# A differential attention layer: the heads' norm factors begun behind each head, the last head's scaling issued later

## The chip, the cores and the metric

The kernel runs on one core of a Trainium2 chip. The metric is the device time of one execution in microseconds, the median of a few runs. The core's engines take their instructions in order, each from its own queue: TensorE (PE, with its weight loads, PEld), VectorE (DVE), ScalarE (ACT), GpSimd (POOL) and SyncE (SP, which issues DMAs). An instruction that waits for another engine holds everything behind it in its own queue.

## The reference

One layer of a streaming encoder for two groups with the same weights: a prompt of 512 tokens and a sample of 64 tokens, 576 in all, with width 1024. It computes

```
h = x + W_out [ GDN(n) ; DiffAttn(n) ],    n = rmsnorm(x)
h = h + MemCrossAttn(rmsnorm(h), memory K/V)
h = h + W2 relu(W1 rmsnorm(h))^2
y = rmsnorm_final(h)
```

and also gives out the new keys, values and states. GDN is a gated recurrence over chunks of 64 tokens in four heads. The part that the change touches is differential attention, four heads of width 128. A head's output for a query is `softmax(q1·k1) V − lam · softmax(q2·k2) V`, and it is then normalised over its own 128 columns:

```
a  = p[:, :, 0] - lam * p[:, :, 1]
ob = _rmsnorm(a @ v, p['diff_norm']) * (1.0 - lam_init)
_rmsnorm(x, g) = x * rsqrt(mean(x*x) + EPS) * g
```

So each query row of each head has one norm factor, `(mean of squares + EPS)^-0.5`, by which its 128 outputs are multiplied. All is in float32.

## The kernel before

**Tiling and stages.** Rows are handled in tiles of 128 partitions. Products in float32 are made of rounded high and low halves, three products each (high·high, high·low, low·high), all recorded at one line, L107 (L113 is the transpose on PE). Weights come by DMA in slabs of 128x1024 (`raw`); ACT copies the high half (L159, `wh`) and DVE subtracts it to get the low half (L160, `wl`). The stages are: norm and turning of the input, the projections and the recurrence of the prompt, then for each head of differential attention its projection (`diff_project`) and the head itself (`diff_head`), with the recurrence of the sample cut in pieces between the heads; then the projection of memory keys and values, the output projection, memory attention, the feed-forward part and the last norm.

**A head.** `diff_head` treats the 64 sample rows first (`sample_rows`, t = 4): score products into the one bank `g1`, maximum (L1055, L1056) on DVE, exponential on ACT (L1058), the weights' scaling on DVE (L1060 to L1062), a turning product with `both` on PE, and the output product into the one bank `gs`. Then the four prompt tiles t = 0 to 3 do the same with two softmaxes (maxima L1097 and L1098, combination L1102 to L1105). ACT takes the sum of squares of each output (L1114, column t of `so`) and copies the output into `on` (tag `an`, five tiles of 128x128).

**The norm of a head.** `factors()` is two instructions on POOL, a 128x5 multiply-add (L1118) and a power (helper, L206), which turn `so` into `co`. `finish()` multiplies `on` by `co` in one DVE instruction (L1127, 128x640), turns it on PE and scales it on ACT into `od`. For heads 0 to 2 `finish` is handed to the next head, which calls it as `between()` ahead of its second prompt tile (t = 1). For the last head it is called in the memory projection.

**The memory projection.** A loop over the weights of keys, then of values; for each, two halves `f` of the columns and four slabs `kc`. In slab 1 the keys of the half before are turned (`turn_keys`): twice, four transposes into a bank, then `split_turned` with a copy on ACT (L1153) and a subtraction on DVE (L1154, into `At0`, `At1`, `Dt0`, `Dt1`). The last head's `finish()` is called right behind this, at values, f = 0, kc = 1.

**What sets the order.** The program is written stage by stage, and a scheduler in the framework makes each engine's queue from it, by the order in which the code was written, by dependences, by which buffers are free, and by its own idea of how long each instruction takes. Buffers of one tag are reused in turn. `tc.issue_after(x)` holds an instruction behind instruction x in that scheduling. The order is fixed when the program is built; on the chip only waits remain.

Of the kernel before, what the change touches and what calls it, by code (L numbers as in the profile page):

```python
# [11 lines left out]
ALU = mybir.AluOpType  # L12
# [3 lines left out]
P = 128  # L16
# [8 lines left out]
H = 4  # L25
# [12 lines left out]
def hybrid_layer_kernel(  # L38
# [9 lines left out]
    nc = tc.nc  # L48
    V, A, G = nc.vector, nc.scalar, nc.gpsimd
# [33 lines left out]
    def pair(slot, dt=F32):  # L83

        return up.tile([P, 2, 4, T], dt, tag=f"u{slot}", name=nm("u"))
# [6 lines left out]
    def small(tag, shape, bufs=None, dt=F32):  # L92
        tag = SHARED.get(tag, tag)
        bufs = 1 if tag in ("vn", "on", "S", "qz") or tag[:-1] in ("At", "Dt", "Y") else 2
        return sp.tile(shape, dt, tag=tag, name=nm(tag), bufs=bufs)

    def tiny(shape, tag="tiny", bufs=16):
        return tp.tile(shape, F32, tag=tag, name=nm(tag), bufs=bufs)

    def bank(tag="ba"):  # L100
        return ps.tile([P, 512], F32, tag=tag, name=nm(tag), bufs=BANKS[tag])
# [4 lines left out]
    def mm(out, lhsT, rhs, start=True, stop=True, pin=False, skip_group_check=False):  # L106
        i = nc.tensor.matmul(out, lhsT, rhs, start=start, stop=stop, skip_group_check=skip_group_check)  # L107
        if pin:
            tc.keep_in_program_order(i)

    def tr(out, in_, pin=False):
        n = in_.shape[0]
        i = nc.tensor.transpose(out, in_, ident[:n, :n])  # L113
        if pin:
            tc.keep_in_program_order(i)
# [89 lines left out]
    def rpow(out, in_, n=None):  # L205
        G.tensor_tensor(out, in_, bc(nhalf[: in_.shape[0], 0:1], list(in_.shape)), ALU.pow)  # L206
# [419 lines left out]
    def v4(ap, nb):  # L626
        return ap.rearrange("p (h n) -> p h n", h=4)[:, :nb, :]
# [186 lines left out]
    def gdn_scan(c, L, q, S):  # L814

        (_, kb), (cq, qb) = (blocks(typ, c, L) for typ in (1, 0))
        wide = [P, 4, P]

        def each(f, tag="gs"):
            b = bank(tag)  # L820
            for h in range(H):
                f(b[:, h * P : (h + 1) * P], h)
            return v4(b, 4)

        if S is None:
            r = q["vb"]
        else:
            b = each(lambda o, h: mm(o, kb(h), S[:, h, :]))
            r = sb("r", 1)
            V.tensor_tensor(r, q["vb"], b, ALU.subtract)  # L830
        b = each(lambda o, h: mm(o, q["X"][:, h, :], r[:, h, :]))
        vn = sb("vn", 1)
        V.tensor_tensor(vn, b, q["brk"].unsqueeze(2).to_broadcast(wide), ALU.mult)

        def out(o, h):
            if S is not None:
                mm(o, qb(h), S[:, h, :], stop=False)
            mm(o, q["KQ"][:, h, :], vn[:, h, :], start=S is None)

        bo = each(out)  # L840
        b = each(lambda o, h: mm(o, q["kd"][:, h, :], vn[:, h, :]), "ba")
        S = next_state(c, S, b)
        on = sb("on", 1)
        norm = normed(q, 4, [(slice(0, P), bo)], on)
        next(norm)

        def finish():
            with tc.issue_after(summed[min(c + 2, 4)]):
                next(norm, None)
            bt = each(lambda o, h: tr(o, on[:, h, :]))  # L850
            V.scalar_tensor_tensor(cq, bt, gn, zs[:, :, L], ALU.mult, ALU.mult)

        return S, finish
# [60 lines left out]
    S, behind = None, lambda: None  # L914
    prepared = [gdn_prep(*chunks[0])]
    for c, _, L in chunks[:4]:
# [5 lines left out]
        S, behind = gdn_scan(c, L, prepared[c], S)  # L922
# [152 lines left out]
    def diff_head(h, between):  # L1075


        hs = slice(h * P, (h + 1) * P)
        so, co = tiny([P, 5], "ta"), tiny([P, 5], "ta")
        on = small("an", [P, 5, P])  # L1080
        for t in (4, 0, 1, 2, 3):
            if t == 1:
                between()
            q0 = QT[t][0]
            nk = q0 + P if t < 4 else PAST + DEC
            nb = (nk + P - 1) // P
            if t == 4:
                sample_rows(h, hs, so, on)
                continue
            pr = {}  # L1090
            mx, l = tiny([P, 2], "ta"), tiny([P, 2], "ta")
            for c in (1, 0):
                b = bank(f"g{c}")
                for j in range(2):
                    mm(b[:, :nk], qs[h % 2][:, c, q0 : q0 + P], stacked[h][c][j][:, :nk], start=j == 0, stop=j == 1)
                V.memset(b[:64, nk - 64 : nk], -1e30)
                V.tensor_reduce(mx[:, c : c + 1], b[:, :nk], AX.X, ALU.max)  # L1097
                V.tensor_scalar(mx[:, c : c + 1], mx[:, c : c + 1], -0.125, None, ALU.mult)  # L1098
                p = small(f"p{c}", [P, 512])
                A.activation(p[:, :nk], b[:, :nk], AF.Exp, bias=mx[:, c : c + 1], scale=0.125, accum_out=l[:, c : c + 1])  # L1100
                pr[c] = p
            V.reciprocal(l, l)  # L1102
            V.tensor_tensor(l[:, 1:2], l[:, 1:2], nlam, ALU.mult)
            V.tensor_scalar(pr[1][:, :nk], pr[1][:, :nk], l[:, 1:2], None, ALU.mult)
            V.scalar_tensor_tensor(pr[0][:, :nk], pr[0][:, :nk], l[:, 0:1], pr[1][:, :nk], ALU.mult, ALU.add)  # L1105
            bt = bank()
            aT = small("aT", [P, 4, P])
            for kb in range(nb):
                tr(bt[:, kb * P : (kb + 1) * P], pr[0][:, kb * P : (kb + 1) * P])
            A.copy(aT[:, :nb, :], v4(bt, nb))  # L1110
            po = bank("gs")[:, :P]
            for kb in range(nb):
                mm(po, aT[:, kb, :], vtm[:, kb, hs], start=kb == 0, stop=kb == nb - 1)
            A.activation(pr[1][:, :P], po, AF.Square, accum_out=so[:, t : t + 1])  # L1114
            A.copy(on[:, t, :], po)

        def factors():
            G.tensor_scalar(so, so, 1.0 / P, EPS, ALU.mult, ALU.add)  # L1118
            rpow(co, so)

        if h == H - 1:
            factors()

        def finish():
            if h < H - 1:
                factors()
            V.tensor_tensor(on, on, co.unsqueeze(2).to_broadcast([P, 5, P]), ALU.mult)  # L1127
            b, b2 = bank(), bank()
            for t in range(4):
                tr(b[:, t * P : (t + 1) * P], on[:, t, :])  # L1130
            tr(b2[:, :P], on[:, 4, :])
            for src, ts_ in ((b, slice(0, SEQ)), (b2[:, DEC:P], slice(SEQ, T))):
                A.activation(od[:, h, ts_], src, AF.Identity, scale=dn)

        return finish

    finish = lambda: None
    for h in range(H):
# [4 lines left out]
        finish = diff_head(h, finish)  # L1143
# [30 lines left out]
    for w, out in ((w_mem_k, o_mk), (w_mem_v, o_mv)):  # L1174
        dst = tokens
        for f in range(2):
            fs = slice(512 * f, 512 * f + 512)
            bs = [bank("pr") for _ in range(2)]
            for kc in range(4):
                wt = split_weights(w[0, 256 * kc : 256 * kc + 256, fs], [P, 2, 512])  # L1180
                if kc == 1:
                    turn_keys()
                    if out is o_mv and f == 0:
                        finish()
                for k in (2 * kc, 2 * kc + 1):
                    for t in range(2):
                        ts_ = slice(t * P, (t + 1) * P)
                        for j, (wi, x) in enumerate(((0, mh), (0, ml), (1, mh))):
                            mm(
                                bs[t], x[:, k, ts_], wt[wi][:, k % 2, :],  # L1190
                                start=(k == 0 and j == 0), stop=(k == KT - 1 and j == 2),
                            )
            for t in range(2):
                (A.copy if t else V.tensor_copy)(dst[:, t, fs], bs[t])
                if out is o_mv:
                    A.copy(mv[:, t, fs], dst[:, t, fs])
                    V.tensor_tensor(mvl[2 * t + f], dst[:, t, fs], mv[:, t, fs].bitcast(F32), ALU.subtract)
            nc.sync.dma_start(out[0, 0].rearrange("(b p) h d -> p b (h d)", p=P)[:, :, fs], dst[:, :, fs])
            turn_keys = key_turns(f, dst) if out is o_mk else lambda: None
            if out is o_mv and f == 0:  # L1200
                ob = pair(5, F32R)
                for h in range(H):
                    split_to((ob,), od[:, h, :], h, 0)
# [513 lines left out]
```

## Time and profile before

| | us |
|---|---|
| runs | 977.66, 977.60, 976.36 |
| median | 977.60 |
| profiled execution | 977.09 |
| its span | 975.3 |
| PE busy | 960.4 (98%) |
| DVE busy | 689.4 (71%) |
| ACT busy | 536.9 (55%) |
| POOL busy | 66.6 (7%) |

The span is the time between the first and the last instruction of the profiled execution. Busy time is the union of an engine's instructions; the TensorE clock was granted in full. A row of the timeline gives start and duration in us, the engine, the line, the operation with output and inputs by the program's names, and in brackets the idle time ahead of it on its engine with the instruction that ended it. Rows with `x2` and more stand for that many instructions of a kind, one after the other.

### The profile page before, as it was taken

What the parts mean: (1) busy time and instruction counts of PE and PEld (TensorE: products, weight loads), DVE (VectorE), ACT (ScalarE), POOL (GpSimd) and SP (SyncE); (2) the same over time, 40 slices, a digit from 0 to 9 for tenths busy, and PEclk for the clock granted to TensorE, in tenths of its full rate; (3) what the DMA queues carried; (4) which work ended last, traced back from release to release, by engine and by line L of the source; (5) the groups of instructions that cost most, each with busy time, mean ns of one, the idle gap of its engine ahead of it and who ended that gap; (6) DMA issues with size and microseconds to landing.
All of it is one profiled execution on the core that took longest, in us unless ns stands there. A gap on an engine that the chain in (4) does not pass through costs nothing.

```text
span 975.3 us, 16991 instructions
## 1 busy us (share of the span) xinstructions
PE 960.4 (98%) x6399; PEld 889.9 (91%) x6399; DVE 689.4 (71%) x1508; ACT 536.9 (55%) x1218; POOL 66.6 (7%) x158
## 2 busy tenths in 40 slices
PE   9999999998999999999999999999999999999996
PEld 7999998997888878999999999999999999999996
DVE  6655777776867776666657888567867779978674
ACT  6664774533656765435445567665544444545444
POOL 4341020211010000000000000000000000000000
PEclk9999999999999999999999999999999999999999
DMA  7442332120744666341121423332323223322202
GB/s 209 117 138 77 95 125 66 46 64 23 187 122 122 219 182 196 87 130 44 45 65 44 141 69 96 90 88 88 87 81 87 87 87 87 87 87 87 66 23 97
DMA packets 124915, 96.01 MB, mean 98 GB/s; under 512 B 6204, under 2 KB 112846, under 8 KB 124322
## 3 DMA queue, kind: packets, MB, share of 16 engines
q1 hardware_dynamic: 124466, 94.28, 33.6%
q8 instruction: 50, 0.82, 0.4%
q10 hardware_dynamic: 368, 0.66, 0.2%
q14 instruction: 31, 0.25, 0.1%
HBM read 79.93 MB, written 9.75 MB: 92 GB/s over the span
## 4 chain that ended last, share of the span: by engine, by line
PE 58%; issue 2%; DVE 1%; ACT 1%; DMA 0%; POOLq 0%; POOL 0%; ACTq 0%; DVEq 0%; SPq 0%
PE pr L107 37%; PE ba L107 10%; PE g L107 6%; PE gs L107 4%; PE ba L113 1%; DMA raw<-in_w_ff_dram 0%; ACT u L1596 0%; ACT c L1504 0%; DVE u L1552 0%; DVE w2l L1458 0%; ACT c L1503 0%; DVE w L1357 0%; DVE wl L1357 0%; DVE wh L1357 0%; ACT wl L1356 0%
## 5 line engine op out<-in xcount | busy, mean ns | idle before, releaser
L107 PE MATMUL pr<-u,wh 128*128 128x320 f32 (+2 forms) x1240 | 325.9, 341 | 0.1
L107 PE MATMUL pr<-u,wl 128*128 128x256 f32 (+1 forms) x816 | 226.1, 301 | 0.0
L107 PEld LDWEIGHTS pr<-u,wh 128*128 128x128 f32 x1240 | 212.1, 189 | 15.2 <-ACT u L286 0.3
L107 PEld LDWEIGHTS pr<-u,wl 128*128 128x128 f32 x816 | 150.5, 189 | 2.5 <-DVE wl L387 0.2
L160 DVE TENSOR_TENSOR wl<-raw,wh 128x1024 fp32r<-128x1024 f32 x65 | 79.5, 1223 | 56.5 <-ACT wh L159 56.3
L159 ACT CAST wh<-raw 128x1024 fp32r<-128x1024 f32 x65 | 68.2, 1049 | 61.9 <-PE pr L107 46.6
L107 PE MATMUL pr<-u,w2h 128*128 128x320 f32 (+1 forms) x384 | 98.5, 341 | 0.0
L1457 ACT CAST w2h<-r 128x512 fp32r<-128x512 f32 x56 | 34.7, 620 | 87.6 <-PE pr L107 85.4
L107 PE MATMUL pr<-f,w2h 128*128 128x320 f32 (+1 forms) x288 | 74.5, 341 | 0.5 <-DVE u L1546 0.5
L107 PEld LDWEIGHTS pr<-u,w2h 128*128 128x128 f32 x384 | 65.0, 188 | 4.5 <-ACT u L1542 0.3
L107 PE MATMUL pr<-u,w2l 128*128 128x256 f32 (+1 forms) x256 | 65.2, 296 | 0.0
L1544 DVE TENSOR_TENSOR u<-u,pr 128x256 f32<-128x256 f32 x96 | 42.4, 450 | 17.1 <-PE pr L107 16.5
L206 POOL TENSOR_TENSOR tiny<-tiny,nhalf 128x1 f32<-128x1 f32 (+4 forms) x10 | 8.8, 879 | 651.3 <-DVE tiny L1610 514.1
L107 PE MATMUL ba<-u,wl 128*128 128x288 f32 x360 | 52.9, 296 | 0.0
L107 PEld LDWEIGHTS pr<-f,w2h 128*128 128x128 f32 x288 | 48.8, 188 | 4.5 <-issue 1.7
L107 PEld LDWEIGHTS ba<-u,wl 128*128 128x128 f32 x360 | 49.2, 188 | 0.6 <-ACT keep L1494 0.5
L107 PE MATMUL pr<-f,w2l 128*128 128x256 f32 (+1 forms) x192 | 48.9, 295 | 0.0
L107 PEld LDWEIGHTS pr<-u,w2l 128*128 128x128 f32 x256 | 47.0, 189 | 1.5
L1458 DVE TENSOR_TENSOR w2l<-r,w2h 128x512 fp32r<-128x512 f32 x56 | 38.5, 688 | 9.6 <-ACT w2h L1457 9.4
L107 PE MATMUL pr<-wh,u 128*128 128x512 f32 x128 | 41.6, 400 | 0.1
L1503 ACT ACTIVATE c<-c 128x288 f32<-128x288 f32 x48 | 20.6, 443 | 28.5 <-DVE c L1502 28.5
L107 PEld LDWEIGHTS pr<-f,w2l 128*128 128x128 f32 x192 | 35.2, 189 | 1.1
(552 smaller groups left out, 2024.8 us busy)
## 6 DMA issues: line engine op xcount, KB each, us to landing
raw<-in_w_ff_dram SPq DMA_DIRECT2D x36, 512.0 KB
raw<-in_w_in_dram SPq DMA_DIRECT2D x28, 512.0 KB
r<-in_w_ff_dram SPq DMA_DIRECT2D x56, 256.0 KB
raw<-in_w_mem_k_dram SPq DMA_DIRECT2D x8, 512.0 KB
raw<-in_w_mem_v_dram SPq DMA_DIRECT2D x8, 512.0 KB
raw<-in_w_out_dram SPq DMA_DIRECT2D x8, 512.0 KB
raw<-in_w_mem_q_dram SPq DMA_DIRECT2D x8, 512.0 KB
raw<-in_w_mem_o_dram SPq DMA_DIRECT2D x8, 512.0 KB
```

What stands on the lines that cost most here:

```text
L107: i = nc.tensor.matmul(out, lhsT, rhs, start=start, stop=stop, skip_group_check=skip_group_check)
L113: i = nc.tensor.transpose(out, in_, ident[:n, :n])
L159: A.copy(wh, raw)
L160: V.tensor_tensor(wl, raw, wh.bitcast(F32), ALU.subtract)
L206: G.tensor_tensor(out, in_, bc(nhalf[: in_.shape[0], 0:1], list(in_.shape)), ALU.pow)
L1457: A.copy(wh, src)
L1458: V.tensor_tensor(wl, src, wh.bitcast(F32), ALU.subtract)
L1503: A.activation(c, c, AF.Relu)
L1544: V.tensor_tensor(am, am, b, ALU.add)
```

## The change

`factors()` is called at the end of every head, not only of the last; `finish()` holds only the scaling and what follows. `finish` has an argument: where it is given, the scaling on DVE is issued behind that instruction. The last head's call gives the newest instruction of the program at that place, which is the second subtraction of `turn_keys`.

```diff
@@ -1118,13 +1118,11 @@
             G.tensor_scalar(so, so, 1.0 / P, EPS, ALU.mult, ALU.add)
             rpow(co, so)
 
-        if h == H - 1:
-            factors()
-
-        def finish():
-            if h < H - 1:
-                factors()
-            V.tensor_tensor(on, on, co.unsqueeze(2).to_broadcast([P, 5, P]), ALU.mult)
+        factors()
+
+        def finish(behind=None):
+            with tc.issue_after(behind) if behind is not None else ExitStack():
+                V.tensor_tensor(on, on, co.unsqueeze(2).to_broadcast([P, 5, P]), ALU.mult)
             b, b2 = bank(), bank()
             for t in range(4):
                 tr(b[:, t * P : (t + 1) * P], on[:, t, :])
@@ -1181,7 +1179,7 @@
                 if kc == 1:
                     turn_keys()
                     if out is o_mv and f == 0:
-                        finish()
+                        finish(nc.cur_bb.bb.instructions[-1])
```

No instruction is added or removed on any engine. Lines behind the edit have numbers smaller by two (the scaling is L1125, the subtraction of `split_turned` L1152). Since the scheduler works from the code's order, the queues of PE, DVE, ACT and SP come out in another order from the end of head 0 to the turning of the last head's output; from the first product of the output projection on they are alike. On POOL one thing moves: head 0's power stands ahead of the four POOL instructions of the sample's recurrence, where it stood behind them.

The names in the rows below carry a number each: `an` is `on`, the tile that is scaled, `ta` holds the small columns (`so`, `co`, maxima and sums), `p0` and `p1` are softmax weights, `g0` and `g1` score banks, `pr` banks of projections, `ba` other banks, `u` shared tiles.

DVE at the end of head 1, before: from the reciprocal of the next head's sample rows (it stands right behind L1105 of this head's last tile) to the scaling.

```order
L1060 RECIPROCAL ta_630_3570<-ta_630_3570 128x1
L1061 TENSOR_TENSOR ta_630_3570<-ta_630_3570,nlam_2540 64x1
L1096 MEMSET g1_639_3597 64x64
L1062 TENSOR_SCALAR p1_632_3576<-p1_632_3576,ta_630_3570 128x320
L901 SCALAR_TENSOR_TENSOR on_593_3341<-gs_625_3560,gcol_378,u_2_76 128x256
L903 TENSOR_TENSOR u_425_2518<-on_593_3341,u_425_2518 128x4x64
L1006 COPY u_4_78<-pr_692_3838 128x320
L1097 TENSOR_REDUCE ta_637_3595<-g1_639_3597 128x1
L160 TENSOR_TENSOR wl_766_4135<-raw_764_4132,wh_765_4134 128x1024
L1098 TENSOR_SCALAR ta_637_3595<-ta_637_3595 128x1
L1097 TENSOR_REDUCE ta_637_3595<-g0_641_3605 128x1
L1127 TENSOR_TENSOR an_546_3170<-an_546_3170,ta_545_3169 128x640
```

The same place in the change, right behind L1105 of the head's last tile:

```order
L1055 TENSOR_REDUCE ta_629_3571<-g1_631_3573 128x1
L1125 TENSOR_TENSOR an_546_3172<-an_546_3172,ta_545_3171 128x640
L1006 COPY u_4_78<-pr_692_3840 128x320
L901 SCALAR_TENSOR_TENSOR on_593_3343<-gs_625_3562,gcol_378,u_2_76 128x256
L160 TENSOR_TENSOR wl_766_4135<-raw_764_4132,wh_765_4134 128x1024
L903 TENSOR_TENSOR u_425_2518<-on_593_3343,u_425_2518 128x4x64
L1056 TENSOR_SCALAR ta_629_3571<-ta_629_3571 128x1
L982 TENSOR_TENSOR vb_678_3744<-u_4_78,kd_677_3743 128x256
L1060 RECIPROCAL ta_630_3572<-ta_630_3572 128x1
L1061 TENSOR_TENSOR ta_630_3572<-ta_630_3572,nlam_2540 64x1
L193 TENSOR_TENSOR zr_699_3906<-pr_698_3889,zr_699_3906 128x256
L1062 TENSOR_SCALAR p1_632_3578<-p1_632_3578,ta_630_3572 128x320
```

The scaling has moved up past the weight subtraction and the work on the next head's sample rows, so that L1056 and L1060 to L1062 stand behind it, with the weight subtraction L160 between them. At heads 0 and 2 it stands right behind L1055 as well.

PE at the end of head 1, before, behind the scores of this head's tiles: the products of the next head's scores, `g1_639`, and then the last tile's turning and output.

```order
L107 MATMUL g1_639_3597<-Dt0_600_3355,qs_430_2543 128x128
L107 MATMUL g1_639_3597<-Dt1_601_3356,qs_430_2543 128x128
L113 MATMUL ba_590_3327<-ident_79,p0_589_3321 128x128 x4
L113 MATMUL ba_611_3444<-ident_79,u_4_78 128x128 x2
L107 MATMUL pr_692_3838<-u_7_92,wl_688_3808 128x320
L107 MATMUL pr_692_3838<-u_7_92,wh_687_3807 128x320 x2
L107 MATMUL pr_692_3838<-u_7_92,wl_688_3808 128x320
L107 MATMUL gs_592_3334<-u_4_78,aT_591_3328 128x128 x4
```

In the change, `g1_639` stands here, some thirty rows further down the queue, behind 21 projection products that come after the last tile's output:

```order
L107 MATMUL pr_701_3913<-u_6_91,wh_696_3885 128x320 x2
L107 MATMUL g1_639_3599<-Dt0_600_3357,qs_430_2543 128x128
L107 MATMUL g1_639_3599<-Dt1_601_3358,qs_430_2543 128x128
L107 MATMUL pr_701_3913<-u_6_91,wl_697_3886 128x320
L107 MATMUL pr_701_3913<-u_6_91,wh_696_3885 128x320 x2
L107 MATMUL pr_701_3913<-u_6_91,wl_697_3886 128x320
L107 MATMUL ba_633_3584<-both_2546,p1_632_3578 128x128 x3
```

`ba_633`, the turning of the next head's sample weights, has moved with it, from ahead of these projection products to behind them.

DVE at the last head, before:

```order
L160 TENSOR_TENSOR wl_791_4280<-raw_789_4277,wh_790_4279 128x1024
L1154 TENSOR_TENSOR At0_754_4122<-ba_784_4233,u_753_4121 128x512
L1127 TENSOR_TENSOR an_706_3948<-an_706_3948,ta_705_3947 128x640
L200 TENSOR_TENSOR u_810_4403<-u_2_76,u_810_4403 128x576
L1154 TENSOR_TENSOR At1_755_4123<-ba_785_4240,u_753_4121 128x512
L160 TENSOR_TENSOR wl_796_4303<-raw_794_4300,wh_795_4302 128x1024
L1194 COPY u_2_76<-pr_776_4207 128x512
```

and in the change:

```order
L160 TENSOR_TENSOR wl_806_4363<-raw_804_4360,wh_805_4362 128x1024
L1152 TENSOR_TENSOR At0_754_4122<-ba_784_4233,u_753_4121 128x512
L200 TENSOR_TENSOR u_810_4403<-u_2_76,u_810_4403 128x576
L1152 TENSOR_TENSOR At1_755_4123<-ba_785_4240,u_753_4121 128x512
L1152 TENSOR_TENSOR Dt0_756_4124<-ba_800_4324,u_753_4121 128x512
L160 TENSOR_TENSOR wl_809_4381<-raw_807_4378,wh_808_4380 128x1024
L1152 TENSOR_TENSOR Dt1_757_4125<-ba_801_4331,u_753_4121 128x512
L1125 TENSOR_TENSOR an_706_3950<-an_706_3950,ta_705_3949 128x640
```

The scaling (on `an_706`) has moved behind the last split of turned keys (`Dt1_757`), and the splits of the second half of the keys, `Dt0` and `Dt1`, stand closer to those of the first.

## The prediction

> **What bounds the kernel now.** I read the page's table of busy time first, then the chain of waits, then the stretch in which the order of instructions changes (272 to 381 us: from the end of head 0 to the first product of the output projection), as a view by windows (start:end, length, then busy us of PE, PEld, DVE, ACT and POOL, granted clock, DMA share, GB/s).
>
> ```profile
> PE 960.4 (98%) x6399; PEld 889.9 (91%) x6399; DVE 689.4 (71%) x1508; ACT 536.9 (55%) x1218; POOL 66.6 (7%) x158
> PE 58%; issue 2%; DVE 1%; ACT 1%; DMA 0%; POOLq 0%; POOL 0%; ACTq 0%; DVEq 0%; SPq 0%
> 272.00:381.00 109.00, 107.26 (x621) 91.03 (x621) 74.89 (x197) 68.80 (x192) 7.02 (x14) 1.00 0.57 171
> ```
>
> PE is busy for 98% of the span and most of the chain that can be followed is PE. In the stretch PE stands idle for 109.00 − 107.26 = 1.74 us at a granted clock of 1.00. No instruction is added or removed, so two things can happen only: idle PE time goes away (1.74 us at most, 0.18% of the time) or new idle time comes in. Gains are capped, losses are not. DVE, busy 74.89 of 109.00 us, has slack on the average; what counts is whether one of its instructions that PE waits for comes late.
>
> **The last head: a wait taken away.** Its lines in the timeline are (start, duration, engine, line, operation; in brackets the idle time ahead and what ended it):
>
> ```profile
> 352.88 1.16 POOL L206 TENSOR_TENSOR ta<-ta,nhalf 128x5 f32<-128x5 f32 x1
> 354.08 0.83 DVE L1127 TENSOR_TENSOR an<-an,ta 128x640 f32<-128x640 f32 x1 [1.97 <-POOL ta L206]
> 356.09 1.22 DVE L160 TENSOR_TENSOR wl<-raw,wh 128x1024 fp32r<-128x1024 f32 x1
> 357.22 0.68 DVE L1194 COPY u<-pr 128x512 f32<-128x512 f32 x1
> 355.36 0.62 PE L107 MATMUL pr<-wh,u 128*128 128x512 f32 x2
> 356.04 0.61 PE L107 MATMUL pr<-wh,u 128*128 128x512 f32 x2
> 357.36 0.50 PE L107 MATMUL pr<-wl,u 128*128 128x512 f32 x1 [0.71 <-DVE wl L160]
> 357.96 0.73 PE L107 MATMUL pr<-wh,u 128*128 128x512 f32 x2
> ```
>
> The scaling L1127 stands in DVE's queue until POOL has the power at 354.04; DVE idles 1.97 us. Behind it come two splits and a weight subtraction (L160), which ends at 357.31, and PE's product of that low half starts at 357.36. PE's groups of three products follow each other in 0.68 us (355.36 to 356.04), 0.228 each, so the product would have come at 356.04 + 2 × 0.228 = 356.50 without the wait: 0.86 lost. The next pair comes at 357.96 instead of 357.36 + 0.23 = 357.59: 0.37. Together **1.23 us**, the most that can come back. In the change the scaling stands behind the last split, some 4 us later, and waits for nothing; but the second pair of splits moves ahead of it and the two banks of turned keys are then still worked off one after the other, so I leave about 0.3 lost: **−0.9** (bounds −1.25 and 0: nothing, if another wait on DVE stands there instead).
>
> **Heads 0 to 2: a wait added.** By program order, POOL's two instructions now come ahead of the next head's work, and by the queues the scaling moves up with them: it stands right behind the next head's first maximum (heads 1 and 2: L1055; head 0: likewise), where before it stood some ten instructions later and waited for nothing. DVE works in order, so whatever is behind it waits for POOL. Head 1, before:
>
> ```profile
> 302.14 0.54 ACT L1058 ACTIVATE p<-g,ta 128x320 f32<-128x320 f32 x1
> 302.22 0.75 DVE L1105 SCALAR_TENSOR_TENSOR p<-p,ta,p 128x512 f32<-128x512 f32 x1
> 302.83 0.44 PE L107 MATMUL g<-Dt,qs 128*128 128x128 f32 x2 [0.18 <-ACT p L1058]
> 303.49 0.39 DVE L1062 TENSOR_SCALAR p<-p,ta 128x320 f32<-128x320 f32 x1
> 306.34 1.17 POOL L206 TENSOR_TENSOR ta<-ta,nhalf 128x5 f32<-128x5 f32 x1
> 306.65 0.48 DVE L901 SCALAR_TENSOR_TENSOR on<-gs,gcol,u 128x256 f32<-128x256 f32 x1 [2.77 <-PE gs L113]
> 306.98 0.83 PE L107 MATMUL ba<-both,p 128*128 128x128 f32 x6
> 308.43 0.49 DVE L1006 COPY u<-pr 128x320 f32<-128x320 f32 x1
> 309.51 1.23 DVE L160 TENSOR_TENSOR wl<-raw,wh 128x1024 fp32r<-128x1024 f32 x1 [0.39 <-ACT wh L159]
> 309.57 0.28 PE L107 MATMUL pr<-u,wl 128*128 128x256 f32 x1
> 309.92 0.28 PE L107 MATMUL pr<-u,wl 128*128 128x256 f32 x1
> 310.91 0.81 DVE L1127 TENSOR_TENSOR an<-an,ta 128x640 f32<-128x640 f32 x1
> 312.78 0.46 PE L107 MATMUL pr<-u,wh 128*128 128x320 f32 x2
> 313.22 0.46 PE L107 MATMUL pr<-u,wh 128*128 128x320 f32 x2
> ```
>
> The sample rows of the next head were handled while the last tile of this head was: exponential L1058 at 302.14, its scaled weights L1062 at 303.49, and their turn on PE (`ba<-both`) at 306.98 found everything done. `g<-Dt,qs`, the next score product, needs the bank that L1058 reads, and lost 0.18. In the change L1056, which L1058 needs, stands behind the scaling and five more instructions. The power ends at 306.34 + 1.17 = 307.51, the scaling starts at 307.55 and holds DVE to 308.3, then L1006, L901, a weight subtraction of 1.23, L903 and L1056: end near 310.75. L1058 then runs to 311.34, and PE may start `g<-Dt,qs` at 311.49 (0.15 from the end of L1058 to the product: 302.68 to 302.83). PE in the meantime: from 306.98, without the `both` products that now come later, eight pairs at 0.35 (309.57 to 309.92), so 2.80, then five products at 0.44/3 = 0.147 (312.78 to 313.22): it arrives at 310.52. Stall 0.97. Then L1062 ends near 312.66 and `both` is reached at 312.34 with that stall in it: 0.38 with the step to PE. Less the 0.18 of before: **+1.2** (bounds +0.3, when the casts of that weight are late and DVE does L903 and L1056 first; +1.6, when L160 starts late by the 0.39 that it waited before).
>
> Head 2 and its rows:
>
> ```profile
> 327.12 1.16 PE L107 MATMUL gs<-u,aT 128*128 128x128 f32 x8
> 329.05 1.17 POOL L206 TENSOR_TENSOR ta<-ta,nhalf 128x5 f32<-128x5 f32 x1
> 329.69 0.83 PE L107 MATMUL ba<-both,p 128*128 128x128 f32 x6
> 332.10 1.23 DVE L160 TENSOR_TENSOR wl<-raw,wh 128x1024 fp32r<-128x1024 f32 x1 [4.26 <-ACT wh L159]
> ```
>
> From the start of the head's last output product (327.12) POOL's power ends 3.10 later, the scaling 3.9 later, L1056 right behind it at 4.04, L1058 at 4.64, so `g<-X,qs` can start at 4.79. PE passes the products left to it (to 329.69, so 2.57, then six of 512 at 0.228) and is there at 3.94: 0.85. `both` waits for L1062 (5.66) from 5.27: 0.4. Less 0.18 as at head 1: **+1.1** (bounds 0, since DVE idled for 4.26 us in this stretch and other fillers may stand ahead of the product, and +1.6).
>
> Head 0 has the gated recurrence of the sample behind it:
>
> ```profile
> 277.27 0.20 POOL L1118 TENSOR_SCALAR ta<-ta 128x5 f32<-128x5 f32 x1 [5.36 <-ACT p L1114]
> 284.04 1.16 POOL L206 TENSOR_TENSOR ta<-ta,nhalf 128x5 f32<-128x5 f32 x1
> 277.91 0.42 DVE L193 TENSOR_TENSOR zr<-pr,zr 128x256 f32<-128x256 f32 x1 [2.97 <-ACT zr L192]
> 278.25 0.85 DVE L881 TENSOR_TENSOR vn<-gs,tg 64x256 f32<-64x256 f32 x2
> 279.25 0.67 PE L107 MATMUL gs<-S,vb 128*128 128x256 f32 x2
> 279.75 0.59 PE L107 MATMUL gs<-vn,KQ 128*128 128x256 f32 x2
> 281.91 0.83 PE L107 MATMUL ba<-both,p 128*128 128x128 f32 x6
> 282.05 0.42 DVE L805 TENSOR_REDUCE tg<-on 128x2 f32<-128x256 f32 x1 [2.95 <-ACT on L804]
> 284.12 0.85 DVE L812 TENSOR_TENSOR on<-gs,tg 64x256 f32<-64x256 f32 x2 [0.50 <-POOL tg L809]
> 285.12 0.68 PE L107 MATMUL gs<-u,aT 128*128 128x128 f32 x4 [0.63 <-ACT wh L159]
> ```
>
> This is the one place where POOL's power itself moves: from 284.04 to right behind L1118. So POOL is done at 277.55 + 1.17 = 278.72, the scaling holds DVE to 279.5, and L193 and L881, which were at 277.91 and 278.25, come 1.6 to 1.9 later: the products `gs<-vn,KQ` (279.75 before, and five filler products later in the new order, so some 280.45) wait about 0.3. L805 comes behind L1062 and a weight subtraction at about 283.7, and L812, 2.07 behind it, ends at 286.6 where it ended at 284.97. The single bank `gs` is free only then, and `gs<-u,aT` (the profile names the cast for its 0.63, but 284.97 is the later release) stalls 1.3 (PE's arrival near 285.4 is counted without the first 0.3, which is therefore inside the 1.3) instead of 0.63: **+0.6** (bounds 0, when the cast at 285.1 is what PE waits for and it moves ahead too, and +1.6, when the two waits and the later L805 add up).
>
> **What else moves.** The freed places are filled with projection products in another order, which takes some short turns behind transposes off PE: **−0.4** (bounds −1.0 and +0.5; what is idle in the stretch, 1.74 less the 1.23 above, is near 0.5, and the dependent turns that count as busy give the rest). The POOL instructions cost no PE time by themselves: POOL is busy 7.02 of 109 us. Loads issued elsewhere on SP wait for a free buffer as before and the DMA share is 0.57: 0.
>
> **Sum.** −0.9 + 0.6 + 1.2 + 1.1 − 0.4 = +1.6 us on the profiled 977.09 (span 975.3), 978.7. The median of the runs is 977.6, 0.5 above the profiled one; so **979.2 us**, a little slower. Between 975.65 and 979.55, 0.2% on each side of the median, a measurement of this kernel can tell nothing from no change.
>
> **Rivals.**
>
> *A, the lateness runs on (20%).* After `both` comes the first tile of the next head on the same queue: its maxima, exponentials and subtractions are each late by the stall, and at heads 1 and 2 they meet weight subtractions of 1.23. One such subtraction more ahead of what PE needs, at two heads, less the terms' own 0.4 of slack each: 2 × (1.23 − 0.4) = 1.7, so 979.2 + 1.7 = about 981. For it: L160 already stands ahead of L903 and L1056 at head 1. Against it: DVE has 34 idle us in the stretch to catch up.
>
> *B, the other side, faster (22%).* If the scheduler's fillers cover the waits at heads 0 to 2, because PE reaches the score products later than I count, only the last head and the fillers stay: −0.9 − 0.4, so 976.3. The place is `g<-Dt,qs` at heads 1 and 2; it decides when PE arrives more than 0.9 us later than 310.52 and its like. For it: products of one form can take longer (0.73 at 357.96, where 0.61 is usual). Against: 0.12 more is rare among these rows, 0.9 in the dozen products that stand there would need it in most of them, and nothing else holds PE. Since PE idles 1.74 us in all, it cannot get far under 975.9.
>
> *C, no effect (7%).* The power's end and the scaling trade places without touching PE: 977.6, within 0.4. Against it speak 1.97 us that DVE demonstrably loses at the last head.
>
> *D, POOL and DVE in each other's way (5%).* POOL's power of the last head (1.16) now runs while DVE does a 128x576 product and a weight subtraction of 1.22, each with two tiles of SBUF as inputs, instead of beside an idle DVE. If one had to wait for the other, DVE would be up to 1.16 late ahead of the splits, the same 1.23 would be lost at PE, and the sum would be +1.6 + 0.9 = +2.5, near 980.2. In the rows of before, the power took 1.17 beside a busy DVE at head 1 (306.34, with L901 at 306.65) and 1.16 beside an idle one: nothing of it to be seen, though L901 reads only one tile of SBUF and one of PSUM with its column. The Trainium skill, "SBUF — State Buffer", section "Who interferes with whom", states such an exclusion for a DVE instruction with two SBUF inputs beside a GpSimd one that reads SBUF, for the whole instruction; no pair of that kind stands alone in the rows quoted here.
>
> **How the numbers follow.** The forecast, with its own range of 978.0 to 980.4, has 46%; it lies close to the 979.55 bound, so I split it 29% no change that can be measured and 17% slower. A and D are slower (25% together), B is 12% faster and 10% within the bound, C is within. That gives faster 0.12, same 0.46, slower 0.42. The range takes in half of B's lower end and A with something above: 976.4 to 981.6.
>
> **What would show it.** Right: at heads 0 to 2 the scaling (now L1125) starts about 0.04 behind POOL's L206 with an idle DVE of 1 us or more put down to it; `g<-Dt,qs` and its like at head 2 idle about 1 us, put down to ACT's L1058, and `gs<-u,aT` near 285 about 1.3; the 0.71 ahead of `pr<-wl,u` near 357 is gone, and the last scaling has no wait. PE's idle time in the stretch grows from 1.74 to about 3.7, and the first product of the output projection is some 1.6 later. Wrong: no idle time on PE at those products (B), or new idle time behind the first tiles of heads 2 and 3, put down to DVE (A), or DVE's L160 far above 1.23 beside POOL's last power (D).

## The result, and the profile after

The change makes the kernel slower: 980.55 us (median of 7 runs, 979.70 to 981.05) against 977.66 us (7 runs, 976.36 to 978.18), a ratio of 1.003 with a 95% interval of 1.0019 to 1.0042. That is +2.9 us where the prediction said +1.6, and 980.55 where it said 979.2. That lies inside the stated range, but the range was wide enough to hold "no change" and "faster" as well, so the places of the waits below say more than the total does.

The table of busy time and the chain of the profile after:

```profile
PE 960.7 (98%) x6399; PEld 887.8 (91%) x6399; DVE 690.7 (71%) x1508; ACT 536.4 (55%) x1218; POOL 66.7 (7%) x158
PE 90%; ACT 3%; DVE 3%; issue 2%; DMA 1%; POOL 1%; POOLq 0%; SPq 0%; ACTq 0%; DVEq 0%
```

The totals hardly moved. The chain names POOL with 1% now, where it had 0%, but the place is seen only in the stretch whose order changed. I cut it at the same two instructions of PE in both kernels: a transpose during head 0's last tiles, and the first product of the output projection. In the view by windows, before and then after:

```profile
269.20:380.71 111.51, 109.77 (x639) 93.44 (x638) 77.47 (x203) 70.92 (x201) 7.17 (x15) 1.00 0.57 169
```

```profile
268.85:383.51 114.66, 110.98 (x639) 92.46 (x638) 78.84 (x203) 70.39 (x201) 7.31 (x15) 1.00 0.54 165
```

The stretch became 3.15 us longer with the same PE instructions at the same clock. Idle time of PE went from 1.74 to 3.68 us, as the prediction said it would (about 3.7); another 1.21 us stands in time that counts as busy. Outside the stretch the two executions differ as well (863.8 us before, 863.0 after), so lengths of the stretch are a second measure beside the medians, not the same one. The waits of PE there, before and after (us in total, times, longest):

```profile
PE pr L107 <- DVE wl L160: 0.7, 1, 0.7
PE gs L107 <- ACT wh L159: 0.6, 1, 0.6
PE g L107 <- ACT p L1058: 0.2, 1, 0.2
```

```profile
PE g L107 <- ACT p L1058: 1.5, 2, 0.8
PE gs L107 <- DVE vn L881: 0.7, 1, 0.7
PE gs L107 <- DVE on L812: 0.6, 1, 0.6
PE ba L107 <- DVE g L1096: 0.3, 2, 0.2
PE ba L113 <- DVE p L1105: 0.2, 1, 0.2
```

The last head's wait (`pr` on `wl` L160) is gone. At heads 0 to 2 the wait on L1058 has grown, and waits on L881, L812, L1096 and L1105 appear. The one on L812 stands at the product that waited 0.6 for the cast L159 before. The timeline after shows how they come about. Head 0, head 1 and head 2 in turn, each from POOL's power to the product that PE starts late (rows that stand between are left out):

```profile
277.26 1.18 POOL L206 TENSOR_TENSOR ta<-ta,nhalf 128x5 f32<-128x5 f32 x1
278.48 0.82 DVE L1125 TENSOR_TENSOR an<-an,ta 128x640 f32<-128x640 f32 x1 [4.20 <-POOL ta L206]
279.34 0.46 PE L107 MATMUL pr<-u,wh 128*128 128x320 f32 x2
280.55 0.67 PE L107 MATMUL gs<-S,vb 128*128 128x256 f32 x2 [0.75 <-DVE vn L881]
285.52 0.40 PE L107 MATMUL pr<-u,wh 128*128 128x512 f32 x1
286.47 0.68 PE L107 MATMUL gs<-u,aT 128*128 128x128 f32 x4 [0.55 <-DVE on L812]
...
307.04 1.17 POOL L206 TENSOR_TENSOR ta<-ta,nhalf 128x5 f32<-128x5 f32 x1
308.25 0.83 DVE L1125 TENSOR_TENSOR an<-an,ta 128x640 f32<-128x640 f32 x1 [4.19 <-POOL ta L206]
311.25 0.14 DVE L1056 TENSOR_SCALAR ta<-ta 128x1 f32<-128x1 f32 x1
310.89 0.45 PE L107 MATMUL pr<-u,wh 128*128 128x320 f32 x2
311.49 0.53 ACT L1058 ACTIVATE p<-g,ta 128x320 f32<-128x320 f32 x1 [1.19 <-DVE ta L1056]
312.16 0.44 PE L107 MATMUL g<-Dt,qs 128*128 128x128 f32 x2 [0.81 <-ACT p L1058]
312.93 0.31 PE L107 MATMUL pr<-u,wl 128*128 128x320 f32 x1
313.39 0.91 PE L107 MATMUL ba<-both,p 128*128 128x128 f32 x6 [0.15 <-DVE g L1096]
...
336.03 1.17 POOL L206 TENSOR_TENSOR ta<-ta,nhalf 128x5 f32<-128x5 f32 x1
337.24 0.83 DVE L1125 TENSOR_TENSOR an<-an,ta 128x640 f32<-128x640 f32 x1 [2.77 <-ACT u L1023]
337.82 0.40 PE L107 MATMUL pr<-wh,u 128*128 128x512 f32 x1
338.22 0.53 ACT L1058 ACTIVATE p<-g,ta 128x320 f32<-128x320 f32 x1 [0.83 <-DVE ta L1056]
338.89 0.33 PE L107 MATMUL g<-X,qs 128*128 128x128 f32 x1 [0.67 <-ACT p L1058]
```

At all three heads the scaling starts 0.04 us behind the end of POOL's power, after DVE stood idle for 2.77 to 4.20 us. (At head 2 the profile names ACT's L1023, which ended at about the same moment; the power ended at 336.03 + 1.17 = 337.20. Likewise the wait of `both` at 313.39 is put down to the memset L1096, which ends right behind L1062, the instruction whose result `both` takes in.) Behind the scaling come the instructions that PE waits for.

The row of a wait shows less than the wait costs. At head 1 the two products at 310.89 are through at 310.89 + 2 × 0.147 = 311.18, and the next starts at 312.16: 0.98 lost, of which 0.81 is listed as idle. The other 0.17 stands in the busy time of the product ahead. Head 2 gives the same: 338.89 − 337.82 − 0.228 = 0.84 for a listed 0.67. The distance is what to count, also before:

```profile
302.19 0.46 PE L107 MATMUL pr<-u,wh 128*128 128x320 f32 x2
302.83 0.44 PE L107 MATMUL g<-Dt,qs 128*128 128x128 f32 x2 [0.18 <-ACT p L1058]
```

That is 302.83 − 302.19 − 2 × 0.147 = 0.35 lost for a listed 0.18.

### The profile page after: what moved, and what is told of

Its sections match the earlier page's. It is cut to its first block, busy times and chain, and to the rows that moved or that the text cites. A ratio compares the mean times of both kernels' runs of the same rounds, so it can differ in the third digit from the quotient of the medians.

```text
span 977.7 us, 16995 instructions
## 1 busy us (share of the span) xinstructions
PE 960.7 (98%) x6399; PEld 887.8 (91%) x6399; DVE 690.7 (71%) x1508; ACT 536.4 (55%) x1218; POOL 66.7 (7%) x158
## 4 chain that ended last, share of the span: by engine, by line
PE 90%; ACT 3%; DVE 3%; issue 2%; DMA 1%; POOL 1%; POOLq 0%; SPq 0%; ACTq 0%; DVEq 0%
PE pr L107 56%; PE ba L107 11%; PE g L107 11%; PE gs L107 6%; PE ba L113 2%; PE g L113 2%; ACT wh L159 0%; DVE p L459 0%; DMA r<-in_w_ff_dram 0%; DVE u L231 0%; DMA u<-in_x_prompt_dram 0%; DVE wl L160 0%; POOL tiny L206 0%; ACT u L221 0%; PE gs L113 0%
## 5 line engine op out<-in xcount | busy, mean ns | idle before, releaser
L160 DVE TENSOR_TENSOR wl<-raw,wh 128x1024 fp32r<-128x1024 f32 x65 | 79.5, 1224 | 49.4 <-ACT wh L159 49.1
L159 ACT CAST wh<-raw 128x1024 fp32r<-128x1024 f32 x65 | 68.2, 1049 | 60.2 <-PE pr L107 43.6
```

What stands on the lines that cost most here:

```text
L159: A.copy(wh, raw)
L160: V.tensor_tensor(wl, raw, wh.bitcast(F32), ALU.subtract)
```

## The experiments

All times are medians; the runs of before beside them lay at 977.6 to 977.8. Each edit is shown against the kernel of the change.

**The last head alone.** The factors of heads 0 to 2 stay in `finish`, the last head's scaling is issued behind the last split.

```diff
-        factors()
+        if h == H - 1:
+            factors()
 
         def finish(behind=None):
+            if h < H - 1:
+                factors()
```

> Only the last head's part of the change: its scaling is issued behind the last split of the turned keys; the factors of heads 0 to 2 stay in finish(). All queues are those of before but for two rows on DVE and some transposes on PE. Theory (the last head's wait on POOL cost PE 1.2 to 1.4 us, and the change takes it back): 1.3 us faster than before, about 976.3. Rival (what is saved there is lost again at the memory values, where the transposed scaling comes later): within 0.3 us of before.

Measured: 976.81 us against 977.81, ratio 0.9989 (0.998 to 0.9998). The waits of PE in the stretch and its length, in the profile of this run:

```profile
PE gs L107 <- ACT wh L159: 0.6, 1, 0.6
PE g L107 <- ACT p L1058: 0.2, 1, 0.2
269.25:379.48 110.23, 109.29 (x640) 93.44 (x638) 77.43 (x203) 71.00 (x201) 7.18 (x15) 1.00 0.57 171
```

The wait on `wl` is gone and nothing came in its place; the stretch is 111.51 − 110.23 = 1.28 us shorter. So the theory holds, and this half of the change by itself is faster than both kernels, if only by 0.1%.

**The early factors alone.**

```diff
-                        finish(nc.cur_bb.bb.instructions[-1])
+                        finish()
```

> Only the other part: factors begun behind every head, the last head's scaling where it was. Queues are those of the change but for the last head's rows. Theory (the two parts add): slower than the change by what the last head gained, 1.3 us, so about 4.2 us slower than before, near 981.8. Rival (the loss of heads 0 to 2 is one thing with the later place of the scaling): as the change, near 980.5.

Measured: 982.06 us (ratio 1.0044, 1.003 to 1.0057), 1.5 above the change. Within the noise the parts add. In this run's list of waits the last head's is back, at a transpose of turned keys (the three longest of six):

```profile
PE g L107 <- ACT p L1058: 1.4, 2, 0.8
PE ba L113 <- DVE At L1152: 1.2, 1, 1.2
PE gs L107 <- DVE vn L881: 0.7, 1, 0.7
```

**The scaling moved behind the next head's sample rows.** The factors are early, as in the change, but the scaling can't stand ahead of L1062.

```diff
         V.tensor_scalar(p[:, :nk], p[:, :nk], l, None, ALU.mult)
+        scaled[h] = nc.cur_bb.bb.instructions[-1]
...
-                between()
+                between(scaled.get(h))
...
-    finish = lambda: None
+    scaled = {}
+    finish = lambda behind: None
```

> The change, with the scaling of heads 0 to 2 also held behind an instruction: the scaling of the next head's sample weights (L1062). So DVE does the next head's sample rows ahead of it, and the rest of the queues stays near the change's. Theory (DVE blocked by the scaling makes the loss): the waits of PE on L1058, L881 and `both` that the change's trace shows, 0.81 + 0.15 + 0.67 + 0.18 + 0.75 = 2.6 us, go, so about 978.0. Rival (the new order of products on PE makes the loss by itself, whoever waits): at most 0.6 us of it goes, 980 or more.

Measured: 977.46 us against 977.81, ratio 0.9994 (0.9985 to 1.0003): 3.1 us of the change's time is gone, more than the 2.6 that the listed waits make. The waits on L1058 and L881 don't appear in this run's list any more:

```profile
PE gs L107 <- DVE on L812: 0.5, 1, 0.5
PE ba L107 <- DVE p L1062: 0.3, 1, 0.3
269.21:380.69 111.48, 110.45 (x640) 92.68 (x638) 77.63 (x203) 70.13 (x201) 7.23 (x15) 1.00 0.56 169
```

This doesn't settle the rival, that the new order of products on PE makes the loss by itself. The scheduler moved PE's queue along with the scaling: in the trace the score products that waited stand earlier than in the change, by about 25 places at head 0, 7 at head 1 and 4 at head 2. The run shows that the loss goes when DVE isn't held; it takes the runs with a longer power, further down, which leave the order alone, to part the two. A smaller loss stays here: the kernel has the last head's gain and no long waits, and still takes 0.65 us more than the run with the last head's part alone; its stretch has 110.45 us of busy PE where that one has 109.29, and is 1.25 us longer.

**One head at a time**, each on top of the last head's part (976.81).

```diff
-        factors()
+        if h in (0, H - 1):
+            factors()
 
         def finish(behind=None):
+            if h not in (0, H - 1):
+                factors()
```

and the same with 1 and with 2 in place of 0.

> As the run with the last head's part alone (976.8), and the factors of head 0 alone begun early. Theory (each head pays for its own wait): by the change's trace head 0 loses 0.92 + 0.72 where before lost 0.79, so +0.85 over 976.8, some 977.7; with a third of the 1.1 us that the change loses outside these waits, 978.0. Rival (one head carries nearly all of the loss of 3.7 us between that run and the change): 976.8 or 980.5.

> As the run with the last head's part alone (976.8), and the factors of head 1 alone begun early. Theory: 0.98 + 0.31 at the score product and at `both`, less 0.35 + 0.17 of before: +0.8, some 977.6, with its third of the rest 978.0. Rival (one head carries nearly all): 976.8 or 980.5.

> As the run with the last head's part alone (976.8), and the factors of head 2 alone begun early. Theory: 0.84 + 0.39 + 0.32, less 0.35 of before: +1.2, some 978.0, with its third of the rest 978.3. Rival (one head carries nearly all): 976.8 or 980.5.

Measured: 977.69, 977.53 and 977.99, so +0.88, +0.72 and +1.18 over 976.81. The loss is spread over the heads in about the sizes that the change's trace gave (+0.85, +0.8, +1.2); no single head carries it. The three add up to 2.8, while the change lies 3.7 above that run. The interval of each ratio to before is about ±1 us wide, so the missing 0.9 may be that, or the order of products, which comes out a little differently in each of these kernels; this isn't settled. Counted from the runs of before beside each, which lay at 977.81 for the last head's part and at 977.62 here, the steps are +1.07, +0.91 and +1.37, so 3.35 of 2.9 + 1.0 = 3.9: the missing part is within what the medians can tell.

**POOL's part made longer.**

```diff
             rpow(co, so)
+            rpow(co, so)
```

> The change with POOL's power issued twice for each head (the second writes the same values again). The queues of PE, DVE and ACT are those of the change, row by row; POOL's end comes 1.17 us later at each head. Theory (DVE, held by the scaling until POOL ends, is what PE waits for at heads 0 to 2): 1.17 us more at each of the three, +3.5, near 984.0; the last head has slack and pays nothing. Rival (PE's waits have another origin, and POOL's end is only near them in time): less than 1 us more, under 981.5.

Measured: 984.80 us (ratio 1.0076, 1.0061 to 1.0091), +4.25 over the change. The queues of DVE, ACT and PE are those of the change. PE's listed waits grew at the three places from 0.75, 0.81 and 0.67 to these:

```profile
281.78 0.67 PE L107 MATMUL gs<-S,vb 128*128 128x256 f32 x2 [1.99 <-DVE vn L881]
315.56 0.44 PE L107 MATMUL g<-Dt,qs 128*128 128x128 f32 x2 [2.05 <-ACT p L1058]
344.92 0.33 PE L107 MATMUL g<-X,qs 128*128 128x128 f32 x1 [1.91 <-ACT p L1058]
```

That is 1.24 more at each, 3.7 in all: at these three products PE starts later by all that POOL takes longer. Since PE's order is the change's, row by row, the rival of the order can't make this difference. This carries the theory. (The wait on L812, 0.55 in the change, isn't in this run's list; its product came behind the low clock told of next.) The rest of the 4.25 led to the next run, because this profile showed the granted clock at half behind two of these waits (windows of 2 us, the clock is the third number from the end):

```profile
282.00:284.00 2.00, 2.00 (x7) 1.62 (x7) 1.55 (x5) 1.47 (x3) 0.00 (x0) 0.66 0.00 0
284.00:286.00 2.00, 2.00 (x6) 1.55 (x5) 1.15 (x2) 0.76 (x2) 0.00 (x0) 0.50 0.13 16
286.00:288.00 2.00, 2.00 (x15) 1.83 (x15) 1.64 (x6) 0.48 (x1) 1.28 (x4) 0.99 0.70 246
```

**Longer still**, with the power three times, to see whether the clock follows from the waits.

```diff
             rpow(co, so)
+            rpow(co, so)
+            rpow(co, so)
```

> As the run with the power issued twice, but three times. In that run's profile PE's granted clock fell to 0.50 for about 3 us behind two of its three waits of 1.9 to 2.05 us. Theory (a wait of this length brings the lower clock): with waits of about 3.2 us all three do it; 3 x 1.17 more for the waits, and 1.3 to 1.5 us for each stretch at half clock: 988.3 plus up to 4, near 990 to 992. Rival (the low clock there was chance and has nothing to do with the waits): 988.3, and a granted clock of 1.00 behind the waits.

Measured: 991.96 us (ratio 1.0151, 1.0134 to 1.0168). Each of the three waits is some 2.5 longer than in the change, 7.45 in all, and the clock fell behind each of them. What is left of the 11.4 over the change is 4.0, so 1.3 for each stretch of low clock:

```profile
283.41 0.67 PE L107 MATMUL gs<-S,vb 128*128 128x256 f32 x2 [3.24 <-DVE vn L881]
318.38 0.44 PE L107 MATMUL g<-Dt,qs 128*128 128x128 f32 x2 [3.29 <-ACT p L1058]
348.60 0.33 PE L107 MATMUL g<-X,qs 128*128 128x128 f32 x1 [3.15 <-ACT p L1058]
```

```profile
286.00:288.00 2.00, 2.00 (x7) 1.64 (x7) 1.14 (x4) 0.68 (x2) 0.61 (x3) 0.50 0.11 18
320.00:322.00 2.00, 2.00 (x10) 2.00 (x10) 0.29 (x3) 0.48 (x1) 0.00 (x0) 0.50 0.80 213
350.00:352.00 2.00, 2.00 (x8) 1.81 (x8) 1.33 (x5) 0.48 (x1) 0.00 (x0) 0.50 0.07 22
```

**POOL's power left out**, so that the scaling multiplies by the mean square plus EPS in place of the norm factor.

```diff
-            G.tensor_scalar(so, so, 1.0 / P, EPS, ALU.mult, ALU.add)
-            rpow(co, so)
+            G.tensor_scalar(co, so, 1.0 / P, EPS, ALU.mult, ALU.add)
```

> The change without POOL's power: the scaling multiplies by the mean square plus EPS, so the norm of differential attention is left out in part. POOL's part ends 1.17 us earlier at each head; DVE's order is near the change's (the scaling stands right behind L1055 at heads 0 and 2, four rows later at head 1). Theory: the waits of PE on L1058 (0.81, 0.67) and L881 (0.75) go but for small rests, and what is left over the run with the last head's part alone is the new order of products: about 978.0. Rival (POOL's end is not what makes DVE late there): 980 or more.

Measured: 977.12 us (ratio 0.9996, 0.9986 to 1.0005), 3.4 below the change. The waits on L1058 and L881 are not in its list; what remains over the run with the last head's part alone is 0.3. The scheduler moved rows on PE, DVE and ACT here (at head 1 the scaling stands four rows later and the score product that waited about 11 places earlier; at heads 0 and 2 the score products stand within a place or so of where they do in the change). So this run is weaker evidence than the doubled power, which moved none; both say the same.

## Why the prediction was right, and which terms were not

**The direction and the mechanism were right.** The prediction's step "heads 0 to 2: a wait added" is what happened, at the places that it named, and the runs that shift, lengthen and remove the wait all move the time with it. Rival B (the products cover it) fell, since PE lost time at every one of the places; rival C likewise.

**The last head: −0.9 was a little small.** I left 0.3 for waits that would remain. The trace of the single part shows none: 1.28 us back in the stretch, where the bound was 1.25; 1.0 by the medians, 1.5 between the early factors alone and the change.

**Head 2: +1.1 was right; head 1: +1.2 was too much.** At head 2 the stall was forecast as 0.85 and is 0.84, and that of `both` as 0.4 and is 339.79 − 339.17 − 0.228 = 0.39; alone that head cost 1.18. At head 1 the stall was forecast as 0.97 and is 0.98, and that of `both` as 0.38 and is 313.39 − 312.93 − 0.147 = 0.31. But I took off only the 0.18 that the profile of before lists, where by the distance of starts the same product lost 0.35. With that, and the 0.1 to 0.2 that `both` lost before, the waits make about 0.8; alone, the head cost 0.72.

**Head 0: +0.6, measured +0.88 alone, with the places swapped.** I put 0.3 on `vn` and 1.3 on the bank `gs`. By the distances they are 280.55 − 279.34 − 2 × 0.147 = 0.92 and 286.47 − 285.52 − 0.23 = 0.72. The first wait comes at `gs<-S,vb`, one instruction earlier than I had it, and what is lost there is no longer lost at the second. Before, the second place lost 285.12 − 284.10 − 0.23 = 0.79, so the trace gives +0.85. That the three heads' terms add up to 2.9, near the 2.8 of the single runs, is luck in part: head 0 was put too low by about as much as head 1 too high.

**What else moves: −0.4 had the wrong sign.** This is the term that failed. I took the new order of the projection products as a gain of up to the idle time that was left. Two runs have the early factors without the long waits, in orders near the change's though not the same. Over the run with the last head's part alone they take 0.65 us (scaling behind L1062) and 0.3 us (no power) more by the medians, of which the second isn't clear of noise; their stretches are 1.25 and 0.99 us longer. As traced, the projection's products are cut into five more pieces by other work (56 in the change and 51 before; 55 with the scaling behind L1062 and 50 with the last head's part alone). That each cut costs something fits the traces, in which PE's busy time grew, but no run changed that alone, so it stays an explanation that was only argued.

Put together: the waits that the change's trace shows at heads 0 to 2, less those of before, make 0.85 + 0.8 + 1.2 = 2.85. With the last head's −1.0 that is +1.85, where the prediction's terms for the waits make +2.0. So the waits were sized about right, and 1.0 of the measured 2.9 lies outside them, where the prediction had −0.4. The stretch says the same more strongly: 3.15 − (2.85 − 1.28) = 1.6. The order of products is the likely place for this rest; no run shows it by itself.

**Rival A (the lateness runs on)** has the nearest time, about 981, but not by its mechanism: no further long wait on DVE stands behind the first tiles of heads 2 and 3. What is new is one of 0.2 on L1105, at head 2's last tile.

**Rival D (POOL and DVE in each other's way)** can be read off the profile after, where the last head's power runs beside a DVE product with two tiles of SBUF as inputs:

```profile
364.89 1.17 POOL L206 TENSOR_TENSOR ta<-ta,nhalf 128x5 f32<-128x5 f32 x1
365.28 0.76 DVE L200 TENSOR_TENSOR u<-u,u 128x576 fp32r<-128x576 f32 x1 [1.16 <-ACT u L199]
368.95 0.81 DVE L1125 TENSOR_TENSOR an<-an,ta 128x640 f32<-128x640 f32 x1
369.68 0.75 DVE L200 TENSOR_TENSOR u<-u,u 128x576 fp32r<-128x576 f32 x1
```

DVE's product starts 0.39 us into the power, 0.03 behind the cast L199 that it waited for (364.57 + 0.68 = 365.25), ends before the power does, and takes 0.76 where its like without POOL takes 0.75; the power takes its usual 1.17. The Trainium skill, "SBUF — State Buffer", section "Who interferes with whom", lets one of two such instructions block the other for its whole length; for a power of 128x5 this trace doesn't agree, and the measurement decides. Rival D fell. The third row also shows the scaling without a wait, as forecast.

## What to carry to other kernels

Starting a slow helper's work earlier is no gain if the order of the queues then brings its consumer forward too: look where the consumer stands on its in-order engine, and what stands behind it. Here the power came no sooner at heads 1 and 2, but a scaling that nobody needed yet moved ahead of small instructions that PE's next products hung on (L881 at head 0, L1056 at heads 1 and 2). Hold such a consumer behind the work that is urgent (the last head's half of the change does just this, and was worth 1.0 us by itself), and count a wait by the distance of the starts on the engine that waits, not by the idle time listed.

## What the runs showed of the hardware

I had not expected the clock to react to waits of 2 us. With the power doubled, in the profiled execution, waits of 1.99 and 2.05 us were followed by a granted clock of 0.50, and one of 1.91 us was not; with the power tripled, waits of 3.24, 3.29 and 3.15 us all were. The waits of the change, up to 0.81 us, left the clock at 1.00. From the windows of 2 us with the power doubled (0.66, 0.50, 0.99) I work out that the low clock lasted about 0.34 × 2 / 0.5 + 2 + 0.01 × 2 / 0.5 = 3.4 us, and in it PE's work takes nearly twice as long: `gs<-vn,KQ` at 283.64 took 1.06 us where it takes 0.59 in the profile of the change at 281.92:

```profile
283.64 1.06 PE L107 MATMUL gs<-vn,KQ 128*128 128x256 f32 x2
```

```profile
281.92 0.59 PE L107 MATMUL gs<-vn,KQ 128*128 128x256 f32 x2
```

The profiled execution of that run took 986.71 us with a mean clock of 0.994; the three others took 984.40, 984.46 and 985.13 with 0.997, which the change's runs have as well (0.997 to 0.998). The lowest is 3.85 above the change, close to the 3.7 of the waits alone. The Trainium skill, "TensorE: Matmul & The Clock Gate", section "HAM oscillation — how this bites in real kernels", warns of idle gaps over about 3.4 us; here gaps of about 2 us were enough in two cases of three, in the one execution that was traced.
